# Norm's factor on results up to the gates' end, first products as x lands; scan's gate tiles loaded a step ahead, da's loads in order

## The chip, the cores and the metric

The kernel runs on one core of one Trainium2 chip. Its engines work side by side, each through a list of instructions of its own, and wait for each other by semaphores: PE (matrix products, with PEld for the loading of weights), DVE (vector), ACT (scalar functions and copies), POOL (general purpose) and SP, which here only issues DMA transfers. ACT and POOL issue some transfers too. The metric is the time of one execution on the device, in microseconds (us). The kernel before takes 2065.09 us, the median of three runs (2063.13 to 2066.34).

## The reference

One encoder layer over 512 tokens of width 2048 in float32, cut to what the change touches:

```python
h = rmsnorm(x, norm_w)                 # x * rsqrt(mean(x*x) + EPS) * norm_w, per token
u = h @ w_in                           # one projection of h, columns cut into nine pieces
z_ssm, xbc, dt_f, dt_b, q_a, kv_a, z_attn, g_ssm, g_attn = jnp.split(u, cuts, axis=-1)

xbc = jax.nn.silu(dwconv(xbc, conv_w, conv_b))     # 4 taps along the tokens, per channel
dtf = jax.nn.softplus(dt_f + dt_bias_fwd)          # the same for dtb
y = ssd_scan(xs, dtf, a_f, bm, cm) + flipped scan + d_skip * xs
y = y.reshape(b, s, D_SSM) * jax.nn.silu(z_ssm)
y = rmsnorm(y per group of 512 channels, ssm_norm_w)
...                                                # latent attention on q_a, kv_a -> o
merged = sigmoid(g_ssm) * (y @ w_proj_ssm) + sigmoid(g_attn) * (o @ w_proj_attn)
return rmsnorm(x + merged @ w_out, final_norm_w)
```

The factor of the norm is one number for each token. A product is linear in its rows, so `(x * norm_w * r) @ w` can be computed as `(x * norm_w) @ w` and multiplied by `r` afterwards, a token's results by its own factor. Where a result lies with tokens along the partitions, that factor is a scalar per partition; where it lies with channels along the partitions, it is a row of 512 numbers, the same for each partition.

## The kernel before, in words

**Products.** PE gets each float32 matrix as two parts, `h` (the value rounded to the multiplier's format) and `l` (the remainder), and adds three products: h·h, h·l and l·h (`mm3`, lines 168 to 170). `wchunk` makes one weight chunk of 128x1024 ready: SP loads it into `wraw` (line 160), ACT casts it into `wh` (163), DVE subtracts for `wl` (164; POOL does where `ahead` is 0, which before holds for the very first chunks). There are three buffers of each. A product of 2048 input channels with 128 output channels and 512 tokens takes two chunks, 48 matmuls.

**Start.** The four blocks of 128 tokens of x are loaded, ACT sums their squares, DVE and ACT multiply x by 1/rms, PE turns the 64 blocks of 128x128 (line 225), and from PSUM ACT casts `h_h` (229) and DVE subtracts for `h_l` (230), with the norm's weights as scale. Then h lies in SBUF with channels along the partitions, 16 tiles of 128x512.

**Input products.** dt's product first, then the tiles 4, 5, 0, 1, 2, 3 of `xbc` of group 0. After each, DVE and ACT convolve along the tokens (DVE lines 389 to 391) and the tile goes out to DRAM. DVE also makes the sums of quarters of h that the gates need (`h_sums`, lines 710 to 730) and dt's softplus (`dt_make`, lines 282 to 301).

**Gates.** The products with wz, wgs and wga (2048x2048 each) are done by Strassen's scheme in Winograd's form with seven quarter products P1 to P7 for each pair of column blocks; X, Y and `wraw` are tiles of quarters of the weights, and sums of them are made by accumulating transfers, issued on POOL's queue (line 500), or on DVE. Hooks, functions attached to a place such as `(1, "P7")`, exchange quarters of h for their sums and back. The last step of each result is an activation (silu, sigmoid) on ACT and a store to DRAM (`zs_d`, `gs_d`, `ga_d`).

**Scan.** Four groups, each in four chunks `c` of 128 tokens and two halves `q`. B, C and x tiles of the group are loaded from DRAM (lines 894 to 898); `seg_make` loads `da` for both directions (997), sums it up along the chunk (999) and makes the decay; `diag` multiplies, and after the second half `y_norm` loads the gate tile `z` (841), multiplies (842), takes squares and the root, and `y_turn` turns y on PE (852). In the gaps between these steps PE works on a stock of other products (`fill`: xbc of the next group, q and kv, z of the attention). After the scan come attention and the two output projections.

**What sets the order.** PE's order is the program's. On the other engines a scheduler places each instruction at the time it reckons with, and `tc.high_priority(offset=n)` lets it pull an instruction forward; `tc.keep_in_program_order` takes it out of that freedom. SP's queue is in order: a transfer that waits for its buffer holds up those behind it. Memory of one pool may be given to the next (`reuse_waits="tile"`): a tile there waits for the last use of what lay in its place.

## Time and profile before

| | |
|---|---|
| median of three runs | 2065.09 us (2063.13 to 2066.34) |
| profiled execution, its time | 2063.24 us |
| its span in the trace | 2061.4 us |
| mean granted TensorE clock | 0.985 |
| PE busy | 1968.5 us, 95% of the span |
| DVE busy | 1461.8 us, 71% |
| ACT busy | 967.9 us, 47% |
| POOL busy | 317.4 us, 15% |
| bytes moved | 378.56 MB, 184 GB/s on average |

The span runs from the first to the last event of the trace; the time of the profiled execution is 1.8 us longer. A row of an instruction gives its start, its duration, engine, line of the code, operation, result and operands with shape, a count where several stand in a row, and in brackets the idle time before it and what ended it. A row of waits gives who waited for whom, total, count and longest. The stages in the trace: x until 32.8 us, input products until 109.3, gates until 567.6, scan until about 1120, then attention and output.

### The profile page before, as it was taken

What the parts mean: (1) busy time and instruction counts of PE and PEld (TensorE: products, weight loads), DVE (VectorE), ACT (ScalarE), POOL (GpSimd) and SP (SyncE); (2) the same over time, 40 slices, a digit from 0 to 9 for tenths busy, and PEclk for the clock granted to TensorE, in tenths of its full rate; (3) what the DMA queues carried; (4) which work ended last, traced back from release to release, by engine and by line L of the source; (5) the groups of instructions that cost most, each with busy time, mean ns of one, the idle gap of its engine ahead of it and who ended that gap; (6) DMA issues with size and microseconds to landing.
All of it is one profiled execution on the core that took longest, in us unless ns stands there. A gap on an engine that the chain in (4) does not pass through costs nothing.

```text
span 2061.4 us, 24706 instructions
## 1 busy us (share of the span) xinstructions
PE 1968.5 (95%) x9074; PEld 1627.2 (79%) x9074; DVE 1461.8 (71%) x1946; ACT 967.9 (47%) x1351; POOL 317.4 (15%) x337
## 2 busy tenths in 40 slices
PE   6999999999989999998999999999999999999998
PEld 5888888888868787786788878888877777888886
DVE  7976676676669789698687567666676888776342
ACT  6444444444445656445546344444444454443232
POOL 0001010010043152241331101110010201100120
PEclk9999999999999999998999999999999999999999
DMA  5568657656547847686464857783376876865332
GB/s 195 165 179 200 175 124 192 192 116 182 140 162 189 250 124 205 207 226 201 154 183 153 236 156 200 206 219 90 86 210 249 301 248 264 273 217 169 107 118 82
DMA packets 166585, 378.56 MB, mean 184 GB/s; under 512 B 16001, under 2 KB 65281, under 8 KB 165889
## 3 DMA queue, kind: packets, MB, share of 16 engines
q1 hardware_dynamic: 104688, 238.33, 35.4%
q0 software_dynamic: 26944, 92.29, 20.5%
q10 hardware_dynamic: 34832, 46.38, 6.2%
q8 instruction: 71, 1.16, 0.2%
q14 instruction: 50, 0.40, 0.1%
HBM read 325.03 MB, written 98.04 MB: 205 GB/s over the span
## 4 chain that ended last, share of the span: by engine, by line
PE 71%; DVE 13%; DMA 9%; issue 4%; ACT 3%; SPq 1%; POOL 0%; ACTq 0%; DVEq 0%; POOLq 0%
PE P L564 10%; PE P L565 10%; PE P L563 10%; PE f L1492 3%; PE f L1493 3%; PE f L1491 3%; PE za L168 2%; PE za L169 2%; DVE sum L999 2%; PE za L170 2%; PE xbc L168 2%; PE xbc L169 2%; PE xbc L170 2%; DVE wl L164 2%; DMA wraw<-wps 1%
## 5 line engine op out<-in xcount | busy, mean ns | idle before, releaser
L434 DVE TENSOR_TENSOR wl<-X,wh 128x1024 fp32r<-128x1024 f32 x152 | 185.3, 1223 | 84.5 <-ACT wh L433 83.9
L433 ACT CAST wh<-X 128x1024 fp32r<-128x1024 f32 x152 | 159.5, 1053 | 157.7 <-PE P L565 137.7
L164 DVE TENSOR_TENSOR wl<-wraw,wh 128x1024 fp32r<-128x1024 f32 (+2 forms) x148 | 172.7, 1167 | 85.7 <-ACT wh L163 85.3
L163 ACT CAST wh<-wraw 128x1024 fp32r<-128x1024 f32 (+2 forms) x150 | 145.1, 969 | 138.9 <-PE za L169 41.2
L434 DVE TENSOR_TENSOR wl<-wraw,wh 128x1024 fp32r<-128x1024 f32 x74 | 91.5, 1236 | 96.4 <-ACT wh L433 96.2
L168 PE MATMUL xbc<-h_h,wh 128*128 128x512 f32 x384 | 152.6, 397 | 0.0
L170 PE MATMUL xbc<-h_h,wl 128*128 128x512 f32 x384 | 150.5, 392 | 0.0
L169 PE MATMUL xbc<-h_l,wh 128*128 128x512 f32 x384 | 150.3, 391 | 0.0
L434 DVE TENSOR_TENSOR wl<-Y,wh 128x1024 fp32r<-128x1024 f32 x80 | 97.9, 1224 | 72.9 <-ACT wh L433 72.8
L564 PE MATMUL P<-wl,h_h 128*128 128x512 f32 x384 | 149.5, 389 | 0.0
L565 PE MATMUL P<-wh,h_l 128*128 128x512 f32 x384 | 149.5, 389 | 0.0
L563 PE MATMUL P<-wh,h_h 128*128 128x512 f32 x384 | 149.5, 389 | 0.0
L433 ACT CAST wh<-wraw 128x1024 fp32r<-128x1024 f32 x74 | 77.9, 1053 | 144.4 <-PE f L1493 69.3
L433 ACT CAST wh<-Y 128x1024 fp32r<-128x1024 f32 x80 | 84.2, 1054 | 111.7 <-PE P L565 96.8
L564 PE MATMUL P<-wl,S 128*128 128x512 f32 x288 | 112.4, 390 | 0.6 <-DVE wl L434 0.6
L565 PE MATMUL P<-wh,S 128*128 128x512 f32 x288 | 112.1, 389 | 0.0
L563 PE MATMUL P<-wh,S 128*128 128x512 f32 x288 | 112.1, 389 | 0.0
L168 PE MATMUL za<-h_h,wh 128*128 128x512 f32 x256 | 102.0, 398 | 0.0
L170 PE MATMUL za<-h_h,wl 128*128 128x512 f32 x256 | 100.5, 392 | 0.1
L169 PE MATMUL za<-h_l,wh 128*128 128x512 f32 x256 | 100.2, 391 | 0.0
L999 DVE TENSOR_TENSOR_SCAN sum<-da,scn 128x512 f32<-128x512 f32 x64 | 86.7, 1368 | 0.0
L170 PEld LDWEIGHTS xbc<-h_h,wl 128*128 128x128 f32 x384 | 72.6, 189 | 15.5
(634 smaller groups left out, 5187.8 us busy)
## 6 DMA issues: line engine op xcount, KB each, us to landing
wraw<-wi SPq DMA_DIRECT2D x102, 512.0 KB, 4.1
da<-da_d SPq DMA_DIRECT2D x64, 256.0 KB, 4.6
T_wps<-wps POOLq DMA_DIRECT2D x32, 512.0 KB, 6.2
T_wpa<-wpa POOLq DMA_DIRECT2D x32, 512.0 KB, 9.4
wraw<-wo SPq DMA_DIRECT2D x32, 512.0 KB, 3.5
wraw<-wps SPq DMA_DIRECT2D x24, 512.0 KB, 5.2
xbc_d<-xbc ACTq DMA_DIRECT2D x24, 256.0 KB, 3.5
wraw<-wun SPq DMA_DIRECT2D x16, 384.0 KB, 3.1
```

Of the source, the lines that this page charges most:

```text
L163: act.copy(h, raw)
L164: (dve if ahead[0] else pool).tensor_sub(l, raw, h.bitcast(F32))
L168: pe.matmul(out, wh, xh, start=start, stop=False)
L169: pe.matmul(out, wh, xl, start=False, stop=False)
L170: pe.matmul(out, wl, xh, start=False, stop=stop)
L433: act.copy(hi_, raw)
L434: dve.tensor_sub(lo_, raw, hi_.bitcast(F32))
L563: pe.matmul(bs[i], xh, wh, start=(j == 0), stop=False)
L564: pe.matmul(bs[i], xh, wl, start=False, stop=False)
L565: pe.matmul(bs[i], xl, wh, start=False, stop=(j == 7))
L999: dve.tensor_tensor_scan(sums[dd], flat(da), mask, 0.0, ALU.add, ALU.mult)
L1491: pe.matmul(acc, mh, wh, start=(start and k == 0), stop=False)
```

## The change

**Start.** x comes a second time as `xt`, turned on the host: eight chunks of 512 KB, each with two tiles of 128x512, channels along the partitions. The transposes and the multiplication by 1/rms are gone. As each chunk lands in `x_t`, ACT casts `h_h` and DVE subtracts for `h_l`, now from `x_t` times the norm's weights, without 1/rms. Three products (xbc 4, 5, 0) run side by side in the order A, B, C of the string below, with five of their weight chunks loaded between x's chunks. ACT squares each pair of tiles, and POOL adds the squares into `sq_sum`, a tile of 128x1024. After the 32nd step of the three products PE sums them over the partitions (`square_sums`), DVE takes the root (`r4`, four columns, tokens along the partitions), and after the 43rd step PE spreads it to a row for all partitions (`factor`, R). Three matmuls of ones stand ahead of the first product.

**Results times R.** xbc's products are multiplied by R on DVE before the convolution (line 752, into the single tile `v_x`), dt's in `dt_make`, which moves from the input products into the second half of the first gate, and the gates' by `r4` as the scale of their activation. The order of the products is now xbc 4, 5, 0, 1, 2, 3, then dt.

**h back.** The sums of quarters for the gates are made from `x_t`, which DVE first multiplies by the norm's weights in place (16 rows, line 765), and its four quarters are stored. In the last half of the last gate hooks load them again, POOL (x11, x12) or DVE (x21, x22) multiplies by R, and ACT and DVE split them into `h_h` and `h_l`; before, only x21 came back.

**Scan.** `z` is loaded by `z_load`, a step (half a chunk) ahead of its use; the loads of `da` stay in program order; the loads of B, C and x of a group have priority 200 instead of 60. Later, the last product of the first projection's head becomes a piece of its own in the stock that fills attention's gaps.

```diff
-    for t in range(TT - 1):
-        for k in range(8):
-            x_turn(k, t)
...
+        xs = x_t[:, 2 * j:2 * j + 2, :].rearrange("p k t -> p (k t)")
+        nc.sync.dma_start(xs, a["xt"][j])
+        for k in (2 * j, 2 * j + 1):
+            nw = vec[:, V_NORM + k:V_NORM + k + 1]
+            act.activation(h_h[:, k, :], x_t[:, k, :], AF.Copy, scale=nw)
+            dve.scalar_tensor_tensor(h_l[:, k, :], x_t[:, k, :], nw, h_h[:, k, :].bitcast(F32), ALU.mult, ALU.subtract)
+        for i in ([j - 1] if 0 < j < 7 else [6, 7] if j else []):
+            sq = sxq("sq") if i else sq_sum
+            act.activation(sq, x_t[:, 2 * i:2 * i + 2, :].rearrange("p k t -> p (k t)"), AF.Square)
+            if i:
+                pool.tensor_add(sq_sum, sq_sum, sq)
...
+    order = "AAAABBBB" + "AABB" * 2 + "C" * 8 + "A" * 8 + "B" * 8 + "C" * 8
+    for i in together([gemm_steps(p_, win(t), h_h, h_l, w_) for p_, t, w_ in zip(firsts, firsts_i, early)], order):
+        if i == 31:
+            square_sums()
+        if i == 42:
+            factor()
...
+    def xbc_done(i, p_):
+        dve.tensor_mul(v_x, p_, R)
+        o = st("xbc")
+        put(xbc_d[0][i], conv_silu(v_x, (0, 1, 2, 3, 16, 20)[i], o, lambda n: o))
...
-            act.activation(o, o, f)
+            act.activation(o, o, f, scale=r4[:, t:t + 1])
...
+    gates[0].hooks = {(0, "P5"): [h_load("S3", in_order=True), h_new("S3", 1, 0)], (1, "P5"): [dt_make]}
+    gates[2].hooks = {(1, "P1"): [r_load, h_load("x11"), h_scale("x11", 0, pool), h_new("x11", 0, 0)],
+                      (1, "P2"): [h_load("x12"), h_scale("x12", 0, pool), h_new("x12", 0, 1)],
+                      (1, "P3"): [h_load("x21"), h_scale("x21", 1, dve)],
+                      (1, "P7"): [h_new("x21", 1, 0), h_load("x22", "Y"), h_scale("x22", 1, dve)],
+                      (1, "P4"): [h_new("x22", 1, 1)]}
...
-    def y_norm(c, g, y):
-
+    def z_load(c, g):
         z = st("z")
         nc.sync.dma_start(z, zs_d[c][g])
+        return z
...
-        with tc.high_priority(offset=AHEAD):
+        with tc.high_priority(offset=200):
...
-                nc.sync.dma_start(da, src.unsqueeze(0).broadcast_to([P, 4, P]))
+                tc.keep_in_program_order(nc.sync.dma_start(da, src.unsqueeze(0).broadcast_to([P, 4, P])))
...
+                if q == 1:
+                    zs[c] = z_load(c, g)
```

How the order of the instructions moves is shown at three places. The first is DVE's start. Of before (`xt` are the blocks of tokens, `mm`, `pa` and `pb` banks of PSUM with turned blocks):

```order
L191 TENSOR_TENSOR small<-small 128x1
L220 TENSOR_SCALAR xt_290<-xt_290,small 128x1024
L230 SCALAR_TENSOR_TENSOR h_l<-mm,vec,h_h 128x512 x3
L230 SCALAR_TENSOR_TENSOR h_l<-pa,vec,h_h 128x512 x2
L230 SCALAR_TENSOR_TENSOR h_l<-pb,vec,h_h 128x512 x2
```

Of the change, up to the first row that takes the sums of squares (`ss`) from PSUM:

```order
L164 TENSOR_TENSOR wl<-wraw,wh 128x1024
L237 SCALAR_TENSOR_TENSOR h_l<-x_t,vec,h_h 128x512 x4
L164 TENSOR_TENSOR wl<-wraw,wh 128x1024
L237 SCALAR_TENSOR_TENSOR h_l<-x_t,vec,h_h 128x512 x4
L164 TENSOR_TENSOR wl<-wraw,wh 128x1024
L237 SCALAR_TENSOR_TENSOR h_l<-x_t,vec,h_h 128x512 x2
L164 TENSOR_TENSOR wl<-wraw,wh 128x1024
L237 SCALAR_TENSOR_TENSOR h_l<-x_t,vec,h_h 128x512 x2
L164 TENSOR_TENSOR wl<-wraw,wh 128x1024
L237 SCALAR_TENSOR_TENSOR h_l<-x_t,vec,h_h 128x512 x4
L164 TENSOR_TENSOR wl<-wraw,wh 128x1024
L254 TENSOR_SCALAR small<-ss 128x4
```

The 1/rms of each block of tokens no longer stands ahead of h; h's tiles and the weights of three products take turns, and the root follows behind them.

The second place is DVE ahead of the gates, in the last input product. Of before (tile 3 of xbc), from the `wl` of its first chunk to that of its second; `pl` belongs to dt_make:

```order
L164 TENSOR_TENSOR wl<-wraw,wh 128x1024
L389 SCALAR_TENSOR_TENSOR cacc<-xbc,vec,cacc 128x510
L292 SCALAR_TENSOR_TENSOR pl<-pl,u 64x512
L390 SCALAR_TENSOR_TENSOR cacc<-xbc,vec,cacc 128x511
L292 SCALAR_TENSOR_TENSOR pl<-pl,u 64x512
L391 SCALAR_TENSOR_TENSOR cacc<-xbc,vec,cacc 128x511
L292 SCALAR_TENSOR_TENSOR pl<-pl,u 64x512 x2
L164 TENSOR_TENSOR wl<-wraw,wh 128x1024
```

Of the change (dt's product), from behind the `wl` of its first chunk to that of its second; `s_667`, `s_668` and `sq_sum` hold sums of quarters of x, `S_239` to `S_241` are their remainders:

```order
L399 SCALAR_TENSOR_TENSOR xbc<-v_x,vec,xbc 128x511
L442 TENSOR_TENSOR S_241<-s_585,S_241 128x1024
L400 SCALAR_TENSOR_TENSOR xbc<-v_x,vec,xbc 128x511
L732 TENSOR_TENSOR s_667<-x_t 128x1024
L752 TENSOR_TENSOR v_x<-xbc,R 128x512
L737 TENSOR_TENSOR sq_sum<-s_667,x_t 128x1024
L442 TENSOR_TENSOR S_239<-s_667,S_239 128x1024
L734 TENSOR_TENSOR s_668<-x_t 128x1024
L442 TENSOR_TENSOR S_240<-sq_sum,S_240 128x1024
L739 TENSOR_TENSOR s_667<-sq_sum,x_t 128x1024
L398 SCALAR_TENSOR_TENSOR xbc<-v_x,vec,xbc 128x510
L164 TENSOR_TENSOR wl<-wraw,wh 128x1024
```

Seven rows of 128x1024 for the second half of the sums of quarters stand ahead of that `wl` now, where before seven shorter rows stood.

The third place is SP's queue around the scan's first chunks. Of before, the entry (`wi` are weights of the stock's products, BT and CT the scan's B and C):

```order
L160 DMA wraw<-wi 128x1024 x3
L769 DMA Y<-h_x_199 128x1024 x2
L160 DMA wraw<-wi 128x1024 x3
L894 DMA BT<-xbc_d_4_97 128x512
L895 DMA CT<-xbc_d_5_98 128x512
```

Of the change, the entry:

```order
L818 DMA wraw<-h_x_200 128x1024 x2
L160 DMA wraw<-wi 128x1024
L818 DMA Y<-h_x_201 128x1024 x2
L160 DMA wraw<-wi 128x1024 x4
L964 DMA BT<-xbc_d_4_97 128x512
L965 DMA CT<-xbc_d_5_98 128x512
```

Of before, around the first chunk's z:

```order
L997 DMA da_4982<-da_d 128x4x128
L997 DMA da_4986<-da_d 128x4x128
L160 DMA wraw<-wi 128x1024
L997 DMA da_5065<-da_d 128x4x128
L997 DMA da_5069<-da_d 128x4x128
L160 DMA wraw<-wi 128x1024
L997 DMA da_5151<-da_d 128x4x128
L160 DMA wraw<-wi 128x1024
L841 DMA z<-zs_d_0_129 128x512
L997 DMA da_5155<-da_d 128x4x128
```

Of the change, the same stretch:

```order
L1067 DMA da_4945<-da_d 128x4x128
L1067 DMA da_4949<-da_d 128x4x128
L907 DMA z<-zs_d_0_129 128x512
L160 DMA wraw<-wi 128x1024
L1067 DMA da_5030<-da_d 128x4x128
L1067 DMA da_5034<-da_d 128x4x128
L160 DMA wraw<-wi 128x1024
L1067 DMA da_5114<-da_d 128x4x128
L160 DMA wraw<-wi 128x1024
L907 DMA z<-zs_d_0_133 128x512
```

Five loads of `wi` stand ahead of BT instead of six, and z stands some three loads of weights earlier.

More of the change, by code (lines that the diff above doesn't have):

```diff
@@ L245, in win, with factor @@
+    def factor():
+        rp = pc("rp")
+        for t in range(TT):
+            pe.matmul(rp[:, t * P:(t + 1) * P], ones, v_x[:, t * P:(t + 1) * P], start=True, stop=True)
+        act.copy(R, rp)
+        put(r_d, R)
     def win(tile_i):
         return [(a["wi"][tile_i, 0], 0, 8), (a["wi"][tile_i, 1], 8, 8)]
-    def in_gemm(tile_i, n="mm"):
-        return gemm(mm(n), win(tile_i), h_h, h_l)
-    sx = open_pool("sx", reuse_waits="tile")
-    so = open_pool("so", side="right", reuse_waits="tile")
@@ L577, in __init__ @@
             self.ahead = {}
+            self.spare = "ms" if self.made else "u"
         def hook(self, cp, name):
@@ L627, in head, with head_end @@
             self.p1 = (a, b)
[L628 removed]
+        def head_end(self):
+            return self.second(1, self.p1[1], lambda i: sum_tile("p5"), None, "P2b")
         def pair(self, cp, headed=False):
@@ L785, in build @@
+    gates[0].first_columns(0)
+    first_pair = gates[0].pair(0)
+    for _ in range(24):
+        next(first_pair)
+    dv_ = st("dv_")
+    act.copy(dv_, dtp)
+    put(dv_d, dv_)
+    run(first_pair)
+    run(gates[0].pair(1))
+    for p_ in gates[1:]:
         for cp in range(2):
```

254 lines of the change are left out of this document (140 added, 114 removed).

## The prediction

> **What bounds the kernel now.** I read the page first: span, busy shares and the chain that ended last.
>
> ```profile
> span 2061.4 us, 24706 instructions
> PE 1968.5 (95%) x9074; PEld 1627.2 (79%) x9074; DVE 1461.8 (71%) x1946; ACT 967.9 (47%) x1351; POOL 317.4 (15%) x337
> PE 71%; DVE 13%; DMA 9%; issue 4%; ACT 3%; SPq 1%; POOL 0%; ACTq 0%; DVEq 0%; POOLq 0%
> ```
>
> PE is the bound, so this change, which takes no product away, can only win back time in which PE has nothing to do. Next the windows, cut at the stages' ends. Columns: stretch, length, busy time (with starts) of PE, PEld, DVE, ACT and POOL, granted clock, DMA share, GB/s.
>
> ```profile
> 0.00:32.80 32.80, 13.32 (x64) 11.72 (x65) 19.16 (x45) 22.16 (x39) 5.00 (x8) 1.00 0.60 222
> 32.80:109.30 76.50, 76.50 (x340) 63.37 (x339) 71.97 (x80) 37.49 (x45) 1.56 (x2) 1.00 0.53 176
> 109.30:567.60 458.30, 457.68 (x2017) 378.27 (x2016) 314.96 (x304) 218.26 (x244) 40.06 (x47) 1.00 0.64 164
> 567.60:593.00 25.40, 18.01 (x79) 14.38 (x78) 7.35 (x9) 10.52 (x17) 9.06 (x8) 0.80 0.63 209
> 593.00:1120.00 527.00, 499.26 (x2332) 411.89 (x2331) 440.71 (x606) 284.18 (x413) 162.15 (x129) 0.97 0.64 186
> ```
>
> Before 32.80 PE only turns x (64 transposes). Then seven products in 76.50 us, 10.9 each, without a gap, while DVE is busy 71.97 of 76.50: a second engine almost full. The gates lose 0.6 us, the scan's entry 7.4, the scan 27.7. Last, the waits: PE's over the whole span (first two rows) and between 564 and 594 (the others); total, times, longest.
>
> ```profile
> PE mm L225 <- DVE xt L220: 19.4, 4, 11.0
> PE turn L852 <- ACT y L846: 13.9, 4, 8.1
> PE pb L876 <- ACT dec L322: 4.0, 1, 4.0
> PE pb L876 <- DMA BT<-xbc_d: 1.9, 1, 1.9
> ```
>
> **Start, up to the third product.** The 64 transposes and the norm ahead of them go: 32.8 us before the first product. Now h is made from x as it lands, PE starts with three xbc products side by side, and 1/rms is applied to results. The rows of the old start give the durations.
>
> ```profile
> 5.88 1.06 ACT L210 ACTIVATE scr<-xt 128x1024 f32<-128x1024 f32 x1 [2.72 <-DMA xt<-x]
> 7.77 0.17 DVE L824 TENSOR_SCALAR small<-vec 128x8 f32<-128x8 f32 x1 [7.77 <-DMA vec<-vec]
> 19.36 1.03 ACT L163 CAST wh<-wraw 128x1024 fp32r<-128x1024 f32 x1
> 19.43 4.64 POOL L164 TENSOR_TENSOR wl<-wraw,wh 128x1024 fp32r<-128x1024 f32 x2 [18.55 <-ACT wh L163]
> 19.68 2.11 DVE L188 TENSOR_TENSOR small<-small 128x1 f32<-128x1 f32 x1
> 21.83 2.26 DVE L189 TENSOR_TENSOR small<-small 128x1 f32<-128x1 f32 x1
> 24.31 0.16 DVE L191 TENSOR_TENSOR small<-small 128x1 f32<-128x1 f32 x1
> 25.83 1.84 ACT L229 ACTIVATE h_h<-mm,vec 128x512 fp32r<-128x512 f32 x3
> 26.55 2.07 DVE L230 SCALAR_TENSOR_TENSOR h_l<-mm,vec,h_h 128x512 fp32r<-128x512 f32 x3 [1.29 <-ACT h_h L229]
> L164 DVE TENSOR_TENSOR wl<-wraw,wh 128x1024 fp32r<-128x1024 f32 (+2 forms) x148 | 172.7, 1167 | 85.7 <-ACT wh L163 85.3
> ```
>
> vec lands at 7.8 and holds the norm's weights, so the first h is there at 8.4 (0.61 of ACT) and PE starts then, not at 32.8. Three products are 32.8 us; the first eight steps are fed by ACT one h at a time and wait some 4 us, so 46 would be the end, if nothing else came in between. Before, three products end at 32.8 + 32.8 = 65.6.
>
> Something does come in between. POOL now adds seven 128x1024 tiles of squares, and PE stops after the 32nd step until the sum is there. The rows at 19.43 to 24.31 show what POOL does to DVE: a 128x1 TENSOR_TENSOR that takes 0.16 us takes 2.11 and 2.26, each ending with POOL's instruction of 4.64 / 2 = 2.32. They take turns. The new h_l reads x_t and h_h, both in SBUF, where the old one read PSUM, so I count it and wl among what takes turns. From the first addition (7.8 + 4 h at 0.61 + 1 cast and 2 squares at 1.05 = 13.4) the two engines have 12 h_l at 0.69, 4 wl at 1.17 and 7 x 2.32: 8.3 + 4.7 + 16.2 = 29.2, so the sum is there at 42.6. Without turns the last addition follows the last square (ACT: 31.5) at 33.9. After it: the sums 0.6, 16 steps 10.9, R's matmuls 0.6, and PE at half rate after its long wait (a product's 0.23 us are 0.43 behind the gap at 585, below; four us of it cost 2): 42.6 + 14.1 = 56.7. A gain of 8.9; 19.6 without turns.
>
> The Trainium skill ("SBUF — State Buffer", "Who interferes with whom") says that a VectorE instruction with two SBUF inputs and a GpSimd one that reads SBUF block each other for the whole instruction, which speaks against this start. The trace agrees for TENSOR_TENSOR (2.11 us for 0.16); for h_l's form with both inputs in SBUF no row of before shows it. By the rule the sum of squares is there at 42.6, without it at 33.9.
>
> **What is late next: DVE, up to the second gate product.** Four rows of DVE in the last input product, then the loads of the gates' X:
>
> ```profile
> 88.41 1.23 DVE L164 TENSOR_TENSOR wl<-wraw,wh 128x1024 fp32r<-128x1024 f32 x1 [0.32 <-ACT wh L163]
> 89.55 0.74 DVE L389 SCALAR_TENSOR_TENSOR cacc<-xbc,vec,cacc 128x510 f32<-128x510 f32 x1
> 90.21 0.68 DVE L292 SCALAR_TENSOR_TENSOR pl<-pl,u 64x512 f32<-64x512 f32 x1
> 90.81 0.73 DVE L390 SCALAR_TENSOR_TENSOR cacc<-xbc,vec,cacc 128x511 f32<-128x511 f32 x1
> X<-wz SPq DMA_DIRECT2D x8, 512.0 KB, 5.7
> X<-wz POOLq DMA_DIRECT2D x8, 512.0 KB, 8.8
> 107.64 2.02 POOL L500 DMA_DIRECT2D X<-wz  x2 [83.56 <-DVE wl L434]
> 116.87 1.05 ACT L433 CAST wh<-X 128x1024 fp32r<-128x1024 f32 x1 [3.79 <-DMA X<-wz]
> ```
>
> On DVE the work of seven products is queued as one order. Between the wl of the last product's first and second half stand eleven rows (seven 128x1024, three conv steps, one R multiply). Queued back to back, 1.14, 0.66 and 0.60 a row by their starts, they are 7 x 1.14 + 3 x 0.66 + 0.6 = 10.6 us, and PE's half product is 5.4. Walking DVE's and ACT's rows down, each starting when its engine, its input and its buffer (three each for wh and wl) allow it, that wl is 3.7 us late, the gate's X tiles (their memory is freed by the last conv) cost 5.6 more in the first gate product, and the accumulated X 1.6 in the second: 10.9 in all. The row for before is 0.6, with DVE as full. So between 0 and 10.9; I take 6, nearer the walk because it goes by the order. The start is then worth 8.9 - 6 + 0.6 = 3.5 us, and with both ends -1.4 to 9.5; without turns 9.3 to 20.2.
>
> Before, X is accumulated 9 us after its wl and ready 1 us ahead of PE; that is all the slack the walk has.
>
> **Gates.** dt_make moves into the second half of wz. Its rows (26, some 12 us of DVE) fit beside 31 us of slack per 100, but the first waits for a load of R's row that starts only when p1 is stored, and two wl stand behind it: 1 us, between 0 and 3. In the last gate four reloads of h are scaled, two pairs on POOL (4 x 2.3) and two on DVE (4 x 1.2), and split (6 more casts, 6 more wl-like rows, 6 x 2.2). DVE is busy 315 of 458 there; the additions to the Y tiles wait behind POOL's rows but are needed 8 us later. 1 us, between 0 and 4.
>
> **Scan.** Rows from SP's and ACT's queues, the chain of waits, DVE's waits between 655 and 980, and PE's rows behind the longest gap (their starts 0.43 apart, where 0.23 is full speed):
>
> ```profile
> 564.49 5.77 SPq L160 DMA_DIRECT2D wraw<-wi  x3
> 570.35 0.41 SPq L894 DMA_DIRECT2D BT<-xbc_d  x1
> 577.47 0.62 ACT L899 CAST c_h<-CT 128x512 fp32r<-128x512 f32 x1 [5.39 <-DMA CT<-xbc_d]
> 585.02 0.43 PE xbc L168
> 655.67 6.01 DMA z<-zs_d
> 951.37 4.59 DMA z<-zs_d
> DVE y L842 <- DMA z<-zs_d: 10.7, 4, 4.6
> 966.00 1.12 PE L852 MATMUL turn<-cst,y 128*128 128x128 f32 x4 [8.13 <-ACT y L846]
> 970.33 0.63 PE L169 MATMUL qkv<-h_l,wh 128*128 128x512 f32 x1
> ```
>
> BT stood behind the third of the w loads, which starts at 569.9, once a buffer is free; by the order it now stands behind one whose buffer comes free one product quarter earlier: 2.7 us, and PE's waits at the entry (4.0 + 1.9) are that long. Between 0 and 5; I take 2.7.
>
> z moves ahead of two or three w loads and as many da, so it lands before y asks for it. DVE waited 10.7 us for it, four times, three of them on the chain; PE's turns waited 13.9 for what follows from y, and 8.1 of it in the gap at 957 to 966, after which PE ran at half rate for some 3 us more. The rest of the y chain (square, root, five small rows) stays. I take 8 us of the 13.9 and 3, the share of the z waits on the chain. Lower bound 2 (DVE is busy 441 of 527 and takes the next row instead), upper 17. da keeps its two buffers and is still issued a step or more before its sum: 0.
>
> **Sum.** 3.5 + 2.7 + 8 - 1 - 1 = 12.2. The profiled execution took 2063.2 (1.8 outside the span; the median of the three runs is 2065.1, 1.9 higher): 2063.2 - 12.2 = 2051.0.
>
> **Rivals.** *The start is not held by POOL* (0.25). If h_l doesn't take turns, or POOL's rows slip into ACT-bound gaps, the start is worth 9.3 to 20.2, say 14: 2063.2 - (14 + 2.7 + 8 - 2) = 2040.5. For it: ACT, with 26 us of rows, leaves DVE idle between h's. Against: both rows under POOL stretched.
>
> *The z loads were covered* (0.17). DVE fills the wait with other rows, so only 2 of 11 come back: 2063.2 - 6.2 = 2057; with the walk's full 10.9 at the start 2062, no change. For it: four waits of 16 only. Against: three of them lie on the chain.
>
> *POOL's additions are longer, and the start ends later than it did* (0.13), the one on the other side.
>
> ```profile
> L961 POOL TENSOR_TENSOR yo<-yo,tmp x24: 1283/1452/2272, 603.9 to 1047.4; 128x512 f32<-128x512 f32 x24
> ```
>
> An in-place 128x512 addition takes up to 2.27 us beside a busy DVE, so 128x1024 up to 4.5: 7 x 4.5 = 31.8 instead of 16.2. The squares' sum then comes at 58.2, the third product ends at 72.3, 6.7 later than before; with 10.9 at the gates' entry the start loses 17, and the rest wins 8.7: 2071.5. It decides from a sum later than 50 us. Against: the row at 19.43 had DVE beside it too.
>
> **Numbers.** My forecast has 0.45 (2044 to 2058 by itself). The range over all reaches from 2036 to 2066. What a measurement of this kernel can tell from no change is about 0.2%, 4 us: below 2061 faster. From the cases: faster 0.41 + 0.24 + 0.07 = 0.72; the same 0.17; slower 0.11.
>
> **What would show it.** The group of POOL's additions: 2.3 us each, with h_l at more than 0.69 beside them; PE idle some 7 us ahead of the sums, at about 42. The wl of the last product's second half late, and a wait of P's products for X. Entry: BT issued right at the gates' end. PE's row "turn <- ACT y" under 6 us and no wait of DVE for z. It is wrong if the sums come before 36 or after 50, or if the scan's PE waits are what they were.

## The result: 1.2% slower, and the profile after

The changed kernel takes 2090.52 us (median of four runs, 2090.14 to 2095.01), the kernel before 2065.72 us beside it. The ratio is 1.012, with a 95% interval of 1.0104 to 1.0137. Forecast were 2051.0 us, in a range of 2036 to 2066, and only 0.11 for slower.

The head of the page of the changed kernel, then its windows, cut at the stages of the table below (stretch, length, busy time of PE, PEld, DVE, ACT and POOL, granted clock, DMA share, GB/s):

```profile
span 2088.6 us, 24705 instructions
PE 1985.0 (95%) x9040; PEld 1630.2 (78%) x9040; DVE 1489.7 (71%) x1950; ACT 975.2 (47%) x1346; POOL 342.4 (16%) x346
```

```profile
0.00:58.80 58.80, 50.44 (x175) 37.97 (x176) 42.81 (x52) 27.65 (x36) 19.32 (x13) 0.83 0.57 211
58.80:113.10 54.30, 46.67 (x194) 37.75 (x192) 40.24 (x45) 23.84 (x29) 0.00 (x0) 0.94 0.49 167
113.10:247.00 133.90, 132.82 (x577) 109.29 (x578) 92.32 (x87) 63.23 (x69) 14.05 (x16) 0.99 0.71 182
247.00:315.80 68.80, 59.71 (x241) 47.15 (x240) 52.56 (x58) 31.43 (x36) 3.46 (x4) 0.93 0.51 136
315.80:556.10 240.30, 239.89 (x1057) 198.10 (x1056) 172.76 (x160) 117.66 (x128) 32.08 (x28) 1.00 0.64 169
556.10:596.00 39.90, 35.76 (x145) 27.85 (x144) 31.05 (x32) 19.91 (x23) 3.47 (x4) 0.96 0.66 185
596.00:618.30 22.30, 16.71 (x77) 13.62 (x76) 8.76 (x10) 11.76 (x18) 7.75 (x7) 0.85 0.59 190
618.30:1163.40 545.10, 524.00 (x2451) 432.88 (x2449) 448.11 (x619) 297.05 (x431) 164.21 (x130) 0.98 0.65 188
1163.40:2088.60 925.20, 879.02 (x4135) 725.62 (x4133) 601.10 (x892) 382.69 (x579) 98.05 (x145) 0.99 0.62 190
```

PE is busy 16.5 us longer although it has no more to do. Its busy time also counts matmuls at half rate (0.43 us from start to start instead of 0.23), and the clock column shows where: it is below 1.00 in each stretch in which PE has gaps of some length. From 36.1 to 49.7, for example, the granted clock is 0.50. PE's order of products is the same from the gates on, so the two kernels can be laid side by side at the start of PE's matmuls. The gates are 42 quarter products, counted from 0; "entry" is from the gates' end to the scan's first product on B, C and x.

| stretch (us) | before | after | difference |
|---|---|---|---|
| start to the end of three products | 65.6 | 58.8 | -6.8 |
| to the gates' first product | 43.5 | 54.3 | +10.8 |
| gates, products 0 and 1 | 23.1 | 25.1 | +2.0 |
| products 2 to 11 | 108.8 | 108.8 | 0 |
| products 12 to 16 | 54.4 | 68.8 | +14.4 |
| products 17 to 38 | 239.4 | 240.3 | +0.9 |
| products 39 to 41 | 32.6 | 39.9 | +7.3 |
| entry | 25.0 | 22.3 | -2.7 |
| scan, to its last turn of y | 552.4 | 545.1 | -7.3 |
| behind the scan | 916.6 | 925.2 | +8.6 |
| span | 2061.4 | 2088.6 | +27.2 |

So the gains that the forecast named are there: the start, the entry and the scan give 16.8 us. They are lost between the third product and the gates' end, and behind the scan.

**The start.** POOL's additions, then DVE's h_l as a group and one row of it, in the first 45 us:

```profile
L242 POOL TENSOR_TENSOR sq_sum<-sq_sum,sq x7: 2462/2688/3369, 12.9 to 35.5; 128x1024 f32<-128x1024 f32 x7
L237 DVE SCALAR_TENSOR_TENSOR h_l<-x_t,vec,h_h x16: 735/748/2898, 8.6 to 38.7; 128x512 fp32r<-128x512 f32 x16
30.30 9.09 DVE L237 SCALAR_TENSOR_TENSOR h_l<-x_t,vec,h_h 128x512 fp32r<-128x512 f32 x4
```

Four h_l take 9.09 us beside POOL, where the shortest takes 0.74: the two engines take turns, with h_l's form too. What PE waits for in these 45 us, POOL's last additions, and PE's first rows on the sum of squares:

```profile
PE xbc L169 <- DVE h_l L237: 5.0, 5, 1.8
29.26 8.92 POOL L242 TENSOR_TENSOR sq_sum<-sq_sum,sq 128x1024 f32<-128x1024 f32 x3 [0.57 <-ACT sq L240]
41.08 3.41 PE L251 MATMUL ss<-cst,sq_sum 128*128 128x1 f32 x16
```

The sum of squares is there at 38.2, and PE comes to it at 41.1 without a pause in front of it. PE is late because it waited 5.0 us for the stretched h_l, and because it runs at half clock from 36.1 on.

**The last input product and the entry to the gates.** DVE's rows around the wl of dt's second chunk, ACT's ahead of the first X, and PE's wait:

```profile
92.59 1.22 DVE L732 TENSOR_TENSOR s<-x_t 128x1024 f32<-128x1024 f32 x1
...
98.86 1.23 DVE L739 TENSOR_TENSOR s<-sq_sum,x_t 128x1024 f32<-128x1024 f32 x1
...
100.65 1.23 DVE L164 TENSOR_TENSOR wl<-wraw,wh 128x1024 fp32r<-128x1024 f32 x1
109.96 0.58 ACT L847 COPY dv__1021<-dtp 128x512 f32<-128x512 f32 x1 [3.50 <-PE dtp L170]
111.98 2.94 ACT L442 CAST wh<-X 128x1024 fp32r<-128x1024 f32 x3 [0.40 <-ACT xbc L401]
PE dtp L170 <- DVE wl L164: 4.5, 1, 4.5
```

The sums of quarters stand in front of that wl, DVE without a pause, and PE waits 4.5 us. Then ACT waits for the end of the same product to copy it, and the three casts of X stand behind.

**dt_make in the first gate.** SP, DVE and ACT between 240 and 300, in order of time:

```profile
242.17 0.33 SPq L284 DMA_DIRECT2D p<-r_d  x1
248.31 0.69 DVE L285 TENSOR_TENSOR dv__1618<-dv__1618,p 128x512 f32<-128x512 f32 x1 [4.26 <-DMA p<-r_d]
249.61 0.72 ACT L289 ACTIVATE dv__1618<-dv__1618,vec 64x512 f32<-64x512 f32 x1 [4.09 <-DVE dv__1618 L285]
280.52 0.69 DVE L608 TENSOR_TENSOR p<-p,P 128x512 f32<-128x512 f32 x1 [3.71 <-DMA da_d<-p]
290.54 0.59 ACT L537 COPY p<-P 128x512 f32<-128x512 f32 x1 [2.90 <-DMA zs_d<-p]
292.75 2.94 ACT L442 CAST wh<-X 128x1024 fp32r<-128x1024 f32 x3 [0.40 <-ACT u L802]
```

This is one chain through two tiles called p. dt_make borrows p1, the tiles of the gates' results. It gets them when P2's results are stored (the load of R's row starts at 242.17), keeps them until da is stored (280.5), and only then can the gate's next result be written; that one is stored late, so the copy of the next P1 waits (290.5), and three casts of X stand behind it. Each wait stands in the queue of an engine that feeds PE.

**h back in the last gate.** DVE's wl and h_l beside POOL's row, the additions to Y that are issued behind, and ACT waiting for them:

```profile
549.70 3.42 DVE L442 TENSOR_TENSOR wl<-wraw,wh 128x1024 fp32r<-128x1024 f32 x1
552.42 2.96 POOL L828 TENSOR_TENSOR wraw<-wraw,R 128x1024 f32<-128x1024 f32 x1 [0.39 <-DMA wraw<-h_x]
553.15 3.31 DVE L442 TENSOR_TENSOR h_l<-wraw,h_h 128x1024 fp32r<-128x1024 f32 x1
556.39 1.21 DVE L442 TENSOR_TENSOR wl<-Y,wh 128x1024 fp32r<-128x1024 f32 x1
557.90 0.87 POOL L511 DMA_DIRECT2D Y<-wga  x1 [2.51 <-DVE wl L442]
569.96 1.05 ACT L442 CAST wh<-Y 128x1024 fp32r<-128x1024 f32 x1 [3.88 <-DMA Y<-wga]
```

**The scan.** PE's longest wait there: 7.8 us for the turns instead of 13.9, its longest 3.2 instead of 8.1. DVE's waits for z, 10.7 us before, are no longer in the list.

```profile
PE turn L922 <- ACT y L916: 7.8, 4, 3.2
```

### The profile page after: what moved, and what is told of

Its sections match the earlier page's. It is cut to its first block, busy times and chain, and to the rows that moved or that the text cites. A ratio compares the mean times of both kernels' runs of the same rounds, so it can differ in the third digit from the quotient of the medians.

```text
span 2088.6 us, 24705 instructions
## 1 busy us (share of the span) xinstructions
PE 1985.0 (95%) x9040; PEld 1630.2 (78%) x9040; DVE 1489.7 (71%) x1950; ACT 975.2 (47%) x1346; POOL 342.4 (16%) x346
## 3 DMA queue, kind: packets, MB, share of 16 engines
q1 hardware_dynamic: 105840, 242.00, 35.2%
## 4 chain that ended last, share of the span: by engine, by line
PE 66%; DVE 14%; DMA 10%; issue 5%; ACT 4%; POOL 0%; ACTq 0%; SPq 0%; DVEq 0%; POOLq 0%
PE P L575 8%; PE P L576 8%; PE P L574 8%; PE f L1568 3%; PE f L1569 3%; PE f L1567 3%; DVE wl L442 2%; PE za L168 2%; PE za L169 2%; PE xbc L169 2%; PE za L170 2%; PE xbc L168 2%; PE xbc L170 2%; DVE sum L1069 2%; DMA wraw<-wps 2%
## 5 line engine op out<-in xcount | busy, mean ns | idle before, releaser
L163 ACT CAST wh<-wraw 128x1024 fp32r<-128x1024 f32 (+2 forms) x150 | 144.7, 967 | 139.7 <-PE za L169 42.6
L575 PEld LDWEIGHTS P<-wl,h_h 128*128 128x128 f32 x384 | 73.3, 191 | 24.9 <-DVE wl L442 9.7
L169 PEld LDWEIGHTS xbc<-h_l,wh 128*128 128x128 f32 x384 | 74.5, 194 | 22.6 <-DVE h_l L237 7.3
```

Source lines behind the costliest of these rows:

```text
L163: act.copy(h, raw)
L169: pe.matmul(out, wh, xl, start=False, stop=False)
L575: pe.matmul(bs[i], xh, wl, start=False, stop=False)
```

## The experiments

Where a text below gives a span of a stretch, it is read as in the table above, from the one profiled execution of that kernel; medians and ratios are of all its executions. The kernel before had medians of 2064.1 to 2065.8 us beside these runs, with single executions from 2056.3 to 2072.6; ratios are against it. Two kernels below with the same instructions (the scan's edits without and with unused areas in DRAM) take 542.9 and 545.2 us in the scan, so a difference of 2 or 3 us in a stretch far behind an edit need not come from the edit.

### dt_make with tiles of its own

```diff
-        u, pl = (sum_tile("p1") for _ in range(2))
+        u, pl = (sum_tile("pad") for _ in range(2))
```

`pad` are two tiles that the gates' pool has and that nothing used.

> Edit: dt_make's two scratch tiles lie in two tiles of their own (tag pad) and no longer in the two tiles p1 that also carry the gates' results; nothing else changes. In the changed kernel the second half of the first gate (products 12 to 16 of the gates) falls 14.4 us behind. Theory, buffers: the scratch can only start when p1's results are stored (R's row is asked for at 242.2), DVE and ACT stand 4 us each for it, and the gates' next result waits for the store of da (3.7 us) and of z (2.9 us). With tiles of its own dt_make starts two products earlier and nothing waits for the stores: the stretch loses at most 3 us instead of 14.4, 2090.5 - 11.4 = 2079. Rival, rows: the 26 rows on DVE (one reciprocal of 3.35 us), the two table loads on ACT and the casts behind them are what is late, wherever they stand: the stretch still loses 10 or more, 2086 to 2091.

Measured: 2074.68 us, ratio 1.0047 (1.003 to 1.0064). Products 12 to 16 take 54.4 us, as before the change: the 14.4 us are gone there. But 4.8 appear elsewhere, since dt_make itself has moved. With tiles free from the start the scheduler runs dt_make in the first half of the gate, beside X's additions and the new S3:

```profile
136.81 0.69 DVE L285 TENSOR_TENSOR dv__1618<-dv__1618,pad 128x512 f32<-128x512 f32 x1 [1.95 <-DMA pad<-r_d]
```

Products 2 to 11 take 113.6 instead of 108.8. The theory of the buffers holds for the place, and the rows have a price of their own of 4.8; net 9.6 us come back. This run moves dt_make as well as its tiles, so it doesn't yet tell how much of the 14.4 is the tiles; the next run does. The median fell by 15.8, more than these stages explain; most of the rest lies in entry, scan and behind it.

### The same, kept in program order

```diff
-        nc.sync.dma_start(v, dv_d)
-        nc.sync.dma_start(u, r_d)
-        dve.tensor_mul(v, v, u)
+        tc.keep_in_program_order(nc.sync.dma_start(v, dv_d))
+        tc.keep_in_program_order(nc.sync.dma_start(u, r_d))
+        tc.keep_in_program_order(dve.tensor_mul(v, v, u))
```

(with `pad` as above)

> Edit: dt_make with two scratch tiles of its own, as in the first experiment, and its two loads and first row kept in program order, so that it runs in the second half of the first gate, where it was written, instead of the first half, where the scheduler took it. Theory, place: 4.8 us were lost in the first half because dt_make fell together with X's additions and the new S3; in the second half it costs 0 to 2: 2090.5 - 14.4 + 1 = 2077 less what the other stages vary by, 2070 to 2077; products 2 to 17 take 163.2 to 165 (before 163.2, changed 177.6, first experiment 168.0). Rival, rows: the table loads, the reciprocal of 3.35 us and the casts behind them cost some 5 us anywhere in the gates: products 2 to 17 take 167 or more.

Measured: 2081.37 us, ratio 1.008 (1.0061 to 1.0099). Products 2 to 16 take 111.0 + 60.5 = 171.5 us: 8.3 lost, more than the 4.8 of the run above. The rival holds. DVE's and PE's waits between 200 and 270 of this kernel:

```profile
DVE p L608 <- DMA zs_d<-p: 7.1, 1, 7.1
PE P L575 <- DVE wl L442: 5.8, 3, 4.2
```

Here dt's rows delay P2's result, its store starts late, and P3's result, which needs the tile, holds DVE for 7.1 us, the wl of the next product behind it. So dt_make costs 5 to 8 us at both places in the gates that were tried, with tiles of its own; in the kernel before it cost nothing that shows, beside the input products. Of the 14.4 us of the changed kernel, then, some 6 belong to the borrowed tiles and 8 to the rows in the second half, as far as these two runs tell.

### Sums of quarters earlier

```diff
     for i, p_ in zip((4, 5, 0), firsts):
         xbc_done(i, p_)
+        if i:
+            h_sums(i - 4)
     for i in (1, 2, 3):
         p_ = mm("xbc")
-        if i < 3:
-            h_sums(i - 1)
```

The edit puts them behind the first and the second of the three products; the text on record names the second and the third. They stood behind the third and the fourth, where the text names the fourth and the fifth.

> Edit: the two sets of sums of quarters of x (seven rows of 128x1024 each on DVE) are written right behind the second and the third product's results times R, and no longer behind the fourth and the fifth. DVE stands idle for some 14 us between 56 and 80 in the changed kernel. Theory, queue on DVE: the wl of dt's second chunk was 4.5 us late, and the gates' first casts 3.1, because the rows stood there; 10.8 us were lost on dt's product and the entry, and they come back but for 1 or 2: 2090.5 - 9 = 2081, gates start at about 104. Rival, memory: the gates' X tiles lie where the sums and v_x lay and wait for the last convolution anyway; the rows only trade places: 4 us or less come back, 2086 to 2091.

Measured: 2084.82 us, ratio 1.0089 (1.006 to 1.0117). From the third product to the gates it takes 48.4 us instead of 54.3: 5.9 of the 10.8 come back, and the wait of dt's product is gone. What is left stands on ACT:

```profile
103.68 0.58 ACT L847 COPY dv__1021<-dtp 128x512 f32<-128x512 f32 x1 [2.34 <-PE dtp L170]
105.70 2.94 ACT L442 CAST wh<-X 128x1024 fp32r<-128x1024 f32 x3 [0.40 <-ACT xbc L401]
```

The queue on DVE was the cause of the larger part; the rival's bound of 4 us doesn't hold in this stretch. The gates start at 106.8, not at the theory's 104.

### The copy of dt's product behind the casts

```diff
-    act.copy(dv_, dtp)
+    tc.keep_in_program_order(act.copy(dv_, dtp))
```

(with the sums early)

> Edit: the sums of quarters early as in the run with early sums, and ACT's copy of dt's product in program order, behind the casts of the gates' first X tiles. With early sums alone the gates start at 106.8, and ACT's three casts of X stand behind that copy, which waits for the product's end. Theory, queue on ACT: with the copy behind, the casts run ahead and the 4.4 us at the first gate product (3.3 and 1.0, with the half rate behind it) go: gates start at 102 to 103, 4 us less than the run with early sums there, 2080. Rival, memory or transfers: X lands too late for an earlier cast (its loads wait for the memory of v_x and R): nothing comes back there, or it is lost in the next product; 2084.

Measured: 2087.52 us, ratio 1.0104 (1.0084 to 1.0123). The gates start 47.6 us behind the third product, only 0.8 earlier, since the casts also stand behind the last convolution; and products 0 and 1 take 29.5 us instead of 25.7. PE's waits between 85 and 140 of this kernel name the new one:

```profile
PE P L574 <- ACT dv__1021 L847: 3.1, 1, 3.1
```

PE now waits for the bank of PSUM that the copy should have emptied. The theory falls, and what was won was lost in the next product, as the rival had it: the copy stood in the better place.

### h's quarters multiplied on DVE

```diff
-h_load("x11"), h_scale("x11", 0, pool)
+h_load("x11"), h_scale("x11", 0, dve)
```

(x12 the same)

> Edit: x11 and x12 that come back in the last gate are multiplied by R on DVE instead of POOL. In the changed kernel the last three products of the gates fall 7.2 us behind. Theory, turns: POOL's two rows of 2.9 us for x12 hold DVE's wl and h_l (3.42 and 3.31 instead of 1.2), so wl of Y comes 4 us late, the additions to Y are issued behind it and the next product waits 10.5 us for Y. On DVE two rows cost 2.4 us and nothing stretches: 2 to 4 us come back of 7.2, 2087. Rival, loads: the 2 MB of reloads ahead of the weights on SP's queue make Y late: no change, 2090 to 2092 (or a little slower, since DVE has four rows more).

Measured: 2083.17 us, ratio 1.0094 (1.0072 to 1.0117). Products 39 to 41 take 37.5 us: 2.4 of 7.3 come back. No row there is stretched:

```profile
548.22 1.22 DVE L442 TENSOR_TENSOR wl<-wraw,wh 128x1024 fp32r<-128x1024 f32 x1
549.35 1.22 DVE L828 TENSOR_TENSOR wraw<-wraw,R 128x1024 f32<-128x1024 f32 x1
550.57 1.23 DVE L442 TENSOR_TENSOR wl<-Y,wh 128x1024 fp32r<-128x1024 f32 x1
```

The turns are a third of the loss. For the rest this run doesn't tell the loads from DVE's order; the run with all edits and the last run do.

### The scan's edits alone, on the kernel before

```diff
+                if q == 1:
+                    zs[c] = z_load(c, g)
...
-        with tc.high_priority(offset=AHEAD):
+        with tc.high_priority(offset=200):
...
+                tc.keep_in_program_order(nc.sync.dma_start(da, src.unsqueeze(0).broadcast_to([P, 4, P])))
```

> The kernel before with the scan's edits alone: z loaded a step ahead, da's loads in program order, B, C and x of a group with priority 200. Theory: what the changed kernel won between the gates' end and the scan's end (2.7 + 7.3 = 10.0 us) belongs to these edits: 2065.7 - 10 = 2056. Rival: the entry was won by the other order of the loads ahead of it and the gap by a shift against the other transfers; then 0 to 4 us come back, 2062 to 2066. Both theories leave what follows the scan as before, unless its losses (8.3 us more in the changed kernel, with the same order of instructions) follow the scan's edits: then 2062 too, with the scan itself 10 us shorter.

Measured: 2056.3 us, ratio 0.996 (0.9944 to 0.9976). It is the kernel with the lowest median and ratio here. The scan takes 542.9 us, 9.5 less; the entry takes 25.6, not less than the 25.0 before. Behind the scan 917.9. PE's waits of this kernel, from 567 on:

```profile
PE turn L855 <- ACT y L849: 6.3, 4, 1.7
PE pb L879 <- DMA BT<-xbc_d: 3.4, 1, 3.4
```

So the scan's gain belongs to these edits; no run separates the earlier z from the order of da. The priority of B's load gives nothing by itself: SP issues BT at 570.45 here and at 570.35 before, 2.9 and 2.8 us behind the gates' end. In the changed kernel it is issued 0.6 us behind it, so the entry's 2.7 us come from the loads that stand ahead of BT there.

### The squares added on DVE

```diff
-                pool.tensor_add(sq_sum, sq_sum, sq)
+                dve.tensor_add(sq_sum, sq_sum, sq)
```

> Edit: the seven additions of squares (128x1024) run on DVE instead of POOL. In the changed kernel POOL's rows take 2.5 to 3.0 us each, DVE's h_l beside them 2.2 instead of 0.7, PE starts on the sums at 41.1 and the third product ends at 58.8. Theory, turns: the two engines hold each other up; on DVE alone 12 h_l at 0.66, 5 wl and 7 additions at 1.14 are 21.6 us, the sums come some 5 us earlier, and the third product ends at 52 to 55. What follows is fed by DVE's queue and takes part of it back: 2085 to 2090. Rival: DVE, not POOL, is what the first products wait for, and seven rows more on it make h_l later: the third product ends at 58 to 62, 2090 to 2094.

Measured: 2081.54 us, ratio 1.0066 (1.0046 to 1.0087), 9 us less than the changed kernel. (The profiled execution, 2071.32, lies 10 us below this median.) The third product ends at 48.9, 9.9 us earlier, beyond the theory's own range. The first 45 us of this kernel, DVE's additions, PE's sums and PE's wait for h_l:

```profile
L242 DVE TENSOR_TENSOR sq_sum<-sq_sum,sq x7: 1217/1219/1222, 12.8 to 33.9; 128x1024 f32<-128x1024 f32 x7
L251 PE MATMUL ss<-cst,sq_sum x16: 250/250/271, 35.2 to 36.9; 128*128 128x1 f32 x16
PE xbc L169 <- DVE h_l L237: 0.6, 1, 0.6
```

On POOL an addition took 2.69 us (median) and an h_l beside it up to 2.90; on DVE the addition takes 1.22 and h_l 0.75, and PE's sums start at 35.2 instead of 41.1. PE waits 0.6 us for h_l instead of 5.0, and the granted clock stays at 1.00 from 30.0 to 48.9, where it fell to half in the changed kernel. The rival is right that PE waited for DVE's h_l, but not that more rows on DVE make it later. The engine that was almost free was the dear one.

### All edits together

Squares on DVE, early sums, the copy in order, dt_make with tiles of its own and in order, quarters on DVE, and two of them a product later:

```diff
-                      (1, "P2"): [h_load("x12"), h_scale("x12", 0, pool), h_new("x12", 0, 1)],
-                      (1, "P3"): [h_load("x21"), h_scale("x21", 1, dve)],
+                      (1, "P2"): [h_load("x12")],
+                      (1, "P3"): [h_scale("x12", 0, dve, True), h_new("x12", 0, 1), h_load("x21")],
```

(`True` keeps the rows in program order; x21 is scaled at P7)

> All together: squares added on DVE, sums of quarters early, dt's copy behind the casts of X, dt_make with tiles of its own and in order, h's quarters multiplied by R on DVE, and x12 and x21 multiplied and split one product later. Theory: each stage gives what its own run gave: third product at 53 to 58, gates' start at 98 to 103, products 2 to 17 in 164, the last three products of the gates with 2 to 5 lost instead of 7.2, gates' end at 562 to 570 (before 567.4, changed 596.0), and the scan as in the changed kernel: 2046 to 2056. Rival: the rows taken away from one place fall on another (DVE full up to the gates, Y late again at the end): gates' end at 575 or later, 2060 or more. The kernel before with the scan's edits alone has 2056.3.

Measured: 2076.66 us, ratio 1.0053 (1.0038 to 1.0067). The gates start at 96.7, their last three products take 32.6 as before the change, and they end at 569.8, but the entry takes 29.9 us. SP's queue there:

```profile
568.70 8.42 SPq L160 DMA_DIRECT2D wraw<-wi  x5
577.17 0.44 SPq L966 DMA_DIRECT2D BT<-xbc_d  x1
```

x21, split late, holds two of the three wraw buffers, so the loads ahead of BT come late, and BT behind them. The gates' end lies in the theory's range and not in the rival's (575 or later), but the total lies in the rival's. The span is 10.5 us longer than before the change: the start wins 17.9, and 5.5 go again ahead of the gates, 5.4 in products 0 and 1, 9.4 in products 2 to 16, 4.9 at the entry and 10.8 behind the scan, while the scan wins 7.6. The last products show what made Y late: ACT waits 0.8 us for Y here, 10.5 in the changed kernel and 6.8 with the quarters on DVE alone, with as many bytes reloaded. So it was the place of x12's rows and not the amount of the loads.

### Four edits, and what lies in DRAM

The four edits are squares on DVE, early sums, dt_make with tiles of its own, and quarters on DVE, each as in its diff above.

> The changed kernel with the four edits that each gave something: squares added on DVE, sums of quarters early, dt_make with two tiles of its own, h's quarters multiplied on DVE; the places in which the run with all edits was worse (dt's copy behind the casts, dt_make in order, x12 and x21 a product later) as in the change. Theory, stage by stage from the runs: third product at 48, gates' start at 96 to 97, 25.5 to product 2, 113.6 to product 12 (dt_make in the first half), 54.4 to 17, then 174.3 + 65.3 + 37.5 and 22 to the scan's first product, 543.5 and some 923: 2054 to 2058 of time. Rival: DVE, emptied at the start, is filled in the gates, and the sum of single gains isn't reached: 2065 or more.

Measured: 2063.53 us, ratio 0.9997 (0.9981 to 1.0013), between the theory's range and the rival's. Each stage came within 2.4 us of its forecast (the last products 38.6, the scan 545.8); the profiled execution took 2060.39, so the median lies on the far side of it.

The 8.6 us behind the scan were tried in two ways: the kernel before with the scan's edits and the change's unused areas in DRAM, and the kernel with four edits with its new areas behind all others. "The run before this one" means the kernel before with the scan's edits in the first text below, and in the second the run with four edits.

```diff
-    h_d = {w: scratch(f"h_{w}", 2048) for w in ("x21", "S3")}
+    h_d = {w: scratch(f"h_{w}", 2048) for w in ("x11", "x12", "x21", "x22", "S3")}
...
-        "x": c(inp["x"][0]), "pos": c(inp["positions"]), ...
+        "x": c(inp["x"][0]), "xt": c(inp["x"][0].T.reshape(...)...), "pos": c(inp["positions"]), ...
```

> Edit: the kernel before with the scan's edits, plus what the change adds in DRAM and nothing that uses it: the input xt is declared behind x, and three more areas of 1 MB stand among the scratch areas for the quarters of h. No instruction changes. Open question: in the changed kernel what follows the scan takes 925.2 us where before takes 916.6, with the same order of instructions on every engine; there the loads of w_proj_ssm take 6.2 us instead of 5.2 (median), those of the normed y 7.9 instead of 5.5, and all nine kernels built on the change so far show 920 to 927, both built without it 917 to 918. Theory, place in DRAM: the same tensors lie elsewhere, and their loads are slower for it: the stretch behind the scan takes 921 or more, 2060 to 2064 in all. Rival, history: it hangs on how the engines and queues come out of the earlier stages: 917 to 919 and 2056.

> As the run before this one, but the change's new input and areas in DRAM stand behind all others, so that what was there before lies where it lay: xt last of the inputs, the areas for x11, x12 and x22 and R last of the scratch areas, dt's product in the place of the area that the change dropped. No instruction changes. Theory, place in DRAM: the stretch behind the scan goes back to 917 or 918, 5 to 6 us less than in the run before, and the total is 2049 to 2053. Rival, history: the stretch and the total stay within 2 us of the run before this one.

Measured: 2058.34 us, ratio 0.998 (0.9966 to 0.9993), with 918.1 us behind the scan; and 2062.3 us, ratio 0.9998 (0.9983 to 1.0014), with 923.6. More areas in DRAM don't lengthen the stretch, and moving them to the end doesn't shorten it (920.6 in the run with four edits). In these two runs the place in DRAM doesn't show as the cause.

### x12 behind P3's rows, x21 as in the change

```diff
-                      (1, "P2"): [h_load("x12"), h_scale("x12", 0, dve), h_new("x12", 0, 1)],
-                      (1, "P3"): [h_load("x21"), h_scale("x21", 1, dve)],
+                      (1, "P2"): [h_load("x12")],
+                      (1, "P3"): [h_scale("x12", 0, dve, True), h_new("x12", 0, 1), h_load("x21"), h_scale("x21", 1, dve)],
```

(on the kernel with four edits)

> The kernel with the four edits (squares on DVE, early sums, dt_make with tiles of its own, h's quarters on DVE), and x12 multiplied behind the rows of product P3 instead of ahead of them, in program order. In the run with all edits this brought the last products of the gates back to 32.6 us as before, but the scan's entry took 29.9 instead of 22, since BT stood behind six loads of w whose buffers x21 held; here x21 stays as in the change and BT stands behind four. Theory: what delays Y is only where the rows of x12 stand on DVE: the last products take 33 to 35 instead of 38.6, the entry 22 to 25, in all 3 to 5 us less than the run with four edits, 2058 to 2061. Rival: what the rows of x12 don't take there, they take at the entry: the two stretches together stay at 60 to 62 and the time within 2 us of 2063.

Measured: 2057.31 us, ratio 0.9973 (0.9958 to 0.9989). The last products take 32.6 and the entry 21.9, both at the theory's good end or a little beyond, as the total is. The windows of these two stretches:

```profile
531.00:563.60 32.60, 32.60 (x146) 27.00 (x144) 28.37 (x29) 20.08 (x23) 2.59 (x3) 1.00 0.69 189
563.60:585.50 21.90, 17.71 (x78) 13.97 (x77) 11.85 (x13) 12.61 (x19) 8.03 (x7) 0.84 0.72 242
```

PE has no gap in the first, with all four quarters of h reloaded, multiplied and split in it. This is a form of the whole change that is faster than the kernel before; the scan's edits alone (0.996) are not slower than it, with far less; the intervals of the two overlap.

## Why the prediction was wrong, step by step

**The start, up to the third product: the number near, the path another.** Forecast 56.7, measured 58.8; the sums were to be there at 42.6, and PE begins with them at 41.1. h_l does take turns with POOL, which no row before could show for its form, so the rule of the Trainium skill ("SBUF — State Buffer", "Who interferes with whom") held here. The rival "the start is not held by POOL" falls, and so does the one on the other side: POOL's rows took 2.69 us, not 4.5. But PE was to stand some 7 us until POOL had the sum, and it didn't. POOL had it at 38.2; PE came later than that, since it had waited 5.0 us for h_l and ran at half clock for 13.6 us, where I had counted four. The step from the sums to the third product's end took 17.7 us, not 14.1. That the two errors nearly cancel is luck.

**DVE up to the second gate product: the order right, the size wrong.** The term was 6, between 0 and 10.9. It measured 10.8 on dt's product and the gates' start and 2.0 in the gates' first two: 12.8 more than before, beyond the upper end. The wl of dt's product was late as the walk down the queues had it (3.7 us, measured 4.5). The walk's 5.6 us for the X tiles is not what the trace shows: the first three casts of X start behind ACT's copy of dt's product and the last convolution, not behind X's loads. What the walk lacked is that copy, which waits for PE and holds the casts, and the half rate behind each gap: between the third product and the gates the clock is 0.94. So the walk's total was nearer than my discount, but in part for another reason than it gave.

**Gates: the step that failed.** "1 us, between 0 and 3" for dt_make and "1 us, between 0 and 4" for h's return. They measured 14.4 and 7.3. I priced dt_make's first wait and its rows against free time on DVE, but not what the borrowed tiles do at their other end: p1 was free for dt_make late, and came back late for the gates' results, and each of these waits stood in a queue ahead of casts and wl. The first experiment takes that chain away and 14.4 go, with 4.8 reappearing as the price of the rows elsewhere; the second keeps dt_make in the second half, and 8.3 stay lost without the borrowed tiles. So the rows alone cost more than my upper end of 3, and the tiles came on top. For h's return I forecast additions to Y "needed 8 us later"; x12's rows, stretched by POOL or not, stood ahead of Y's wl, the additions to Y stand behind that wl, and the slack was gone: ACT waits 10.5 us for Y. On DVE instead of POOL, x12's rows still cost 4.9; behind the rows of the next product they cost nothing there. DVE's slack per 100 us says nothing on this; I should have walked down the queues, as I did for the rows ahead of the gates.

**Scan: right.** Forecast 2.7 at the entry and 8 in the scan; measured 2.7 and 7.3, and 9.5 for the scan's edits alone on the kernel before. DVE's waits for z are gone, and the rival "the z loads were covered" falls. PE's row "turn <- ACT y" was to be under 6 us and is 7.8, so somewhat less came back of that wait than the sign asked for. The entry's gain came as forecast from the loads ahead of BT; the priority alone gave none.

**Behind the scan: not forecast.** 8.6 us with the same order of instructions on every engine. Medians of the time from issue to landing, before (first) and after, of the same loads behind 1130:

```profile
wraw<-wps SPq DMA_DIRECT2D x24, 512.0 KB, 5.2
xraw<-yn_x SPq DMA_DIRECT2D x6, 512.0 KB, 5.5
```

```profile
wraw<-wps SPq DMA_DIRECT2D x24, 512.0 KB, 6.2
xraw<-yn_x SPq DMA_DIRECT2D x6, 512.0 KB, 7.9
```

PE waits longer at the same places. The kernels built on the change show 919.9 to 927.4 us there, those built on the kernel before 916.6 to 918.1. These are single profiled executions, but the two groups don't overlap. The place in DRAM was tried and doesn't show as the cause; what it is stays open.

**The sum.** -6.8 + 10.8 + 2.0 + 14.4 + 0.9 + 7.3 - 2.7 - 7.3 + 8.6 = 27.2 us of span. The forecast was -12.2, so 39.4 us are missing. The gates have 20.6 of them (22.6 instead of 2), the stretch behind the scan 8.6, the rows ahead of the gates 7.4 (12.8 instead of my 6 less the 0.6 of before), the start 2.1, and entry and scan 0.7.

## What to carry to other kernels

When work is moved to a place with idle time on its engine, follow the buffers it borrows to their next user and the rows queued behind each of its waits; the share of idle time prices only the rows. Work on an idle engine isn't free when its rows stretch those of a busy one: here the stage with seven additions took 9.9 us longer with them on POOL than on DVE. And of a change with many parts, try the cheap local one alone: the scan's edits, a few lines, gave as much as the best form of the whole change that was tried.

## What was not expected of the hardware

Beside POOL, DVE's rows with two inputs in SBUF stretched to whole instructions of POOL in three forms: h_l from 0.74 to 2.90 us, wl from 1.22 to 3.42, h_l of the last gate from 1.22 to 3.31. The first was expected, the two in the last gate were not. POOL's own rows grew too, from 2.46 to 3.37 for the same addition. The granted clock fell to half at 36.1 in the start although PE's pauses just before were only 0.5 and 1.8 us long, and with one more pause of 1.2 us it stayed there for 13.6 us. And the same loads, in the same order, took 1.0 to 2.4 us longer (medians) in a later stage whose instructions hadn't changed, for a reason that these runs don't show.
